# Column sums of a decoder trunk's norms written one item later than the split of their operand

## The chip, the cores and the metric

The kernel runs on one core of one Trainium2 chip. The metric is the device time of one execution in microseconds (us); lower is better. Matrix products run on TensorE (PE in the profile, its weight loads PEld), elementwise work on VectorE (DVE) and ScalarE (ACT), and all transfers between HBM and on-chip memory are issued by SyncE (SP).

## The reference

One layer of a hybrid decoder trunk, in float32, over 2048 tokens and 16 meta tokens put in front, 1024 channels:

```python
h = concat([meta, x])                       # (2064, 1024)
u = rmsnorm(h, mix_norm_g)
p = u @ w_in                                # 1024 -> 1792
p_pool, p_bval, p_bgate, p_cgate, p_cx = split(p)
y_a = pool_mixer(p_pool, ...)               # causal mean over windows 2, 4, 8, 16
y_b = conformer(p_bval, p_bgate, ...)       # gate, causal conv of 31 taps, LayerNorm over 256 channels, silu, matmul
y_c = rg_lru(p_cgate, p_cx, ...)            # causal conv of 4 taps, gates, linear scan, gelu gate
h = h + concat([y_a, y_b, y_c]) @ w_out
h = h + square(relu(rmsnorm(h, mlp_norm_g) @ w_up)) @ w_down     # 1024 -> 4096 -> 1024
return rmsnorm(h, final_norm_g)[meta:]
```

## The kernel before

Channels lie on the 128 partitions, tokens along the free dimension, so an activation of 1024 channels is eight blocks of 128 channels. The tokens are worked in four chunks of 512 (chunk 0 has the 16 meta tokens too).

Each float32 operand is split into a high part, rounded to the type fp32r, and a low rest: `split` (L109) makes the high part on ScalarE (L110) and the rest on VectorE (L111). A product is then three matmuls: high by high, high by low, low by high. An output block of 128 channels by 512 tokens takes 8 channel blocks x 3 = 24 matmuls (`mm_tile`, L278) into one PSUM bank of the pool pm, which has four. Weights come by DMA into tiles wr and are split into tiles wh, two items ahead.

A norm needs the sum of squares over channels, that is across partitions. VectorE adds the squared blocks into a tile ss (`add_square`, L345 and L346), `colsum` splits ss into a tile hl (one buffer) and multiplies it with a matrix of ones on TensorE: two matmuls, L327 for the high part and L328 for the low part, into the pool pb. `rsqrt_of` follows, a square root on ScalarE (L335) and a reciprocal on VectorE (L337).

The program is a list of items, each an output block with its products:

- W: a block of the input projection (14 a chunk), evacuated by `evac_w` (L448, or L454 for chunk 1, whose norm comes late: `gen_late`).
- O: a block of the output projection (8 a chunk). `evac_o` loads the residual into a tile xr (L712), adds it (L714) and squares the sum for norm 2.
- U: the MLP's first product, in four groups a chunk. Chunks 1 to 3 use a scheme with seven products instead of eight (`up_unit`, L302 and L820), with sums of weights that `gen_sums` makes during chunk 0 from loads of `w_up` (L194 to L204).
- D: the second product, 8 blocks a group; the first two run as a pair (`mm_pair`, L292), the second of them only evacuates.

The order is W of chunks 0 and 1 interleaved, O of chunk 0, three more W of chunk 1, then for each chunk its groups of U and D; O of the next chunk and W of the one after come behind the last D of chunks 0 and 1, and O of chunk 3 amid the last D of chunk 2.

All other work is in generators, run by `pump` after each item: it gives the item a budget (5000 for W and O, 3000 for D and for U of chunk 0, 150 for other U), takes the next generator step and subtracts the cost that the step yields, until the credit is used up. A debt is carried over to the next item; a credit is not. Generators in the list `urgent` run first, then the `Mix` of the next chunk, whose lanes take turns. The ones that matter here:

- `gen_x` (chunks 2, 3): eight steps of 1300, one for each block k: load the block into xr (L411), square it, scale and split it into a tile U (L148, L149); then the column sum and the root, 3500. It runs during O of the chunk before the one before.
- `gen_late` (chunk 1): eight loads and squares, 620 each, then the sum and 3500, then the scaling of the held W blocks. It runs during the first U of chunk 0.
- `gen_ln` (each chunk): the LayerNorm, with two column sums one after the other (mean, variance), steps of 1250, 1250, 1250, 3300 and 2500. Its outputs are two of the eight blocks that `gen_ysplit` splits for O.
- `gen_norm2` (`gen_norm2_0` for chunk 0): norm 2, 3300 and then the operands of U.
- `gen_final`: sum and root, 3300, then eight output steps of 660 (L860, output DMA L861).

The tile xr has two buffers, shared by `gen_x`, `gen_late` and `evac_o`. `need` and `need_mix` run a generator to its end at once, before an item that needs it; they don't look at the yielded cost.

The framework orders the instructions of each engine when the program is built: by the order in which they are written, but an instruction whose operands it expects to be late is put behind ready ones, and slots of tiles are given in that order. So a column sum may already stand amid the matmuls of the next item. At run time each engine keeps that order.

Of the kernel before, what the change touches and what calls it, by code (L numbers as in the profile page):

```python
# [31 lines left out]
D = 1024  # L32
KB = D // P
NT = 512
NCH = 4
# [18 lines left out]
BUD0 = 5000  # L54
BUD_U = 150
BUD_D = 3000
GELU_C = 0.7978845608028654


# [20 lines left out]
def build(nc, tc, x0, xr, w_in, w_out, w_fold, w_up, w_down, vecs, gates, pools, pws, out):  # L80
# [25 lines left out]
    def ps_back():  # L106
        return pb.tile([P, NT], F32, name=nm("pb"), tag="pb")
# [207 lines left out]
    def split_new(src):  # L315
        n = src.shape[-1]
        hl = t_("hl", (2, W0), HLB, F32R)
        hi, lo = hl[:, 0, :n], hl[:, 1, :n]
        split(hi, lo, src)
        return hi, lo  # L320

    def colsum(src):

        n = src.shape[-1]
        hi, lo = split_new(src)
        ps = ps_back()
        T.matmul(ps[:, :n], ones, hi, start=True, stop=False)  # L327
        T.matmul(ps[:, :n], ones, lo, start=False, stop=True)  # L328
        return ps
# [23 lines left out]
    for c in range(NCH):  # L353
        o = Chunk()
# [9 lines left out]
    def subs_of(o, full=True):  # L364
        if o.c == 0:
            return [(0, 264), (264, 528)] if full else [(META, W0)]
        return [(0, NT)]
# [35 lines left out]
    def gen_x(o):  # L403

        o.x = []
        if o.c > 1:
            ss = t_("ss", W0, 2)
        for k in range(KB):
            hl = a_tile()
            raw = t_("xr", NT, 2)  # L410
            nc.sync.dma_start(out=raw, in_=xr[o.c - 1, k])  # L411
            if o.c > 1:
                add_square(ss, raw, 0, NT, k == 0)
            split_to(hl[:, 0], hl[:, 1], raw, vc("g1", k))
            o.x.append(hl)
            yield 1300
        if o.c > 1:
            o.rs1 = rsqrt_of([colsum(ss[:, :NT])], subs_of(o), 1.0 / D)
            yield 3500

    def gen_late(o):

        ss = t_("ss", W0, 2)
        for k in range(KB):
            raw = t_("xr", NT, 2)
            nc.sync.dma_start(out=raw, in_=xr[o.c - 1, k])
            add_square(ss, raw, 0, NT, k == 0)
            yield 620
        o.rs1 = rsqrt_of([colsum(ss[:, :NT])], subs_of(o), 1.0 / D)
        yield 3500  # L430
        for kind, i, t in o.held:
            evac_w(o, kind, i, [t])
            yield 700
# [104 lines left out]
    def gen_ln(o):  # L538
        acc = [o.acc[0], o.acc[1]]
        sq = [o.ub[0], o.ub[1]]  # L540
        V.tensor_tensor(out=sq[0][:, :NT], in0=acc[0], in1=acc[1], op=ALU.add)
        ps = colsum(sq[0][:, :NT])
        yield 1250
        for i in range(2):
            V.scalar_tensor_tensor(out=acc[i], in0=ps, scalar=-1.0 / 256.0, in1=acc[i], op0=ALU.mult, op1=ALU.add)
            A.activation(out=sq[i][:, :NT], in_=acc[i], func=AF.Square)
        yield 1250
        V.tensor_tensor(out=sq[0][:, :NT], in0=sq[0][:, :NT], in1=sq[1][:, :NT], op=ALU.add)
        ps = colsum(sq[0][:, :NT])
        yield 1250  # L550
        rs = rsqrt_of([ps], [(0, NT)], 1.0 / 256.0)
        yield 3300
        for i in range(2):
            V.tensor_tensor(out=acc[i], in0=acc[i], in1=rs[:, :NT], op=ALU.mult)
            A.activation(out=acc[i], in_=acc[i], func=AF.Identity, scale=vc("lng", i), bias=vc("lnb", i))
            A.activation(out=sq[i][:, :NT], in_=acc[i], func=AF.Sigmoid)
            V.tensor_tensor(out=acc[i], in0=acc[i], in1=sq[i][:, :NT], op=ALU.mult)
            o.y[2 + i] = acc[i]
        yield 2500
# [157 lines left out]

    def gen_norm2(o):

        rs = rsqrt_of([colsum(o.ss2[:, :NT])], [(0, NT)], 1.0 / D)  # L720
        yield 3300
        o.u2 = ops = {n: [b_tile(), b_tile()] for n in ("B11", "T2", "T3", "T1", "B21", "T4", "B22")}
        free = [("s", SBF)] * SBF + [("t", TB)] * TB
# [53 lines left out]

    def gen_norm2_0(o):

        rs = rsqrt_of([colsum(o.ss2[:, :NT])], [(0, NT)], 1.0 / D)  # L780
        yield 3300
        o.u2 = []
        for k in range(KB):
            raw = t_("s", W0, SBF)[:, :NT] if k % 2 else t_("t", W0, TB)[:, :NT]
            V.scalar_tensor_tensor(out=raw, in0=o.h[k][:, :NT], scalar=vc("g2", k), in1=rs[:, :NT], op0=ALU.mult, op1=ALU.mult)
            t = b_tile()
            split(t[:, 0, :NT], t[:, 1, :NT], raw)
            o.u2.append(t)
            yield 1400
# [63 lines left out]
            add_square(o.ssf, h, s0, s1, j == 0)  # L853

    def gen_final(o, s0, s1):
        rs = rsqrt_of([colsum(o.ssf[:, s0:s1])], [(s0, s1)], 1.0 / D)
        yield 3300
        for k in range(KB):
            h = o.h[k][:, s0:s1]
            V.scalar_tensor_tensor(out=h, in0=h, scalar=vc("gf", k), in1=rs[:, s0:s1], op0=ALU.mult, op1=ALU.mult)  # L860
            nc.sync.dma_start(out=out[o.c, k, :, s0:s1], in_=h)  # L861
            yield 660
# [22 lines left out]
    credit = [0.0]  # L885

    def pump(budget):
        credit[0] = min(credit[0], 0) + budget
        while credit[0] > 0:
            v = step()  # L890
            if v is None:
                break
            credit[0] -= v

# [82 lines left out]
    for n, it in enumerate(items):  # L977
        kind, c, j, (s0, s1) = it
        o = ch[c]
# [140 lines left out]
```

## Time and profile before

| | |
|---|---|
| median of 3 runs | 1968.43 us (1966.31 to 1968.72) |
| the profiled execution | 1969.41 us |
| its span, first to last instruction | 1967.6 us |
| granted TensorE clock, mean | 0.996 |
| busy: PE, DVE, ACT | 1932.1, 1510.1, 1099.2 us |
| column sums (L327, L328) | 20 pairs of matmuls |

A row of the timeline gives the start and the length in us, engine, line, operation, output and inputs, shape and count; in brackets how long the engine was idle before it, and who released it. A row of the waits gives who waited for whom, the us in total, the times and the longest. In a table by stretches, each engine's busy time and count stand before the granted clock, the DMA share and GB/s. PE's busy time counts overlapping matmuls, so its lost time is better read from starts and ends of neighbouring rows.

### The profile page before, as it was taken

The numbers are of one execution on the slowest core, as the hardware profiler recorded it, in microseconds if no ns is written. First come the engines' busy times: TensorE is split into PE (matmuls) and PEld (weight loads), VectorE is DVE, ScalarE is ACT, GpSimd is POOL, SyncE is SP. The second block draws the span as 40 slices with busy tenths as digits, with TensorE's granted clock in tenths as the row PEclk, the third lists the DMA queues.
The fourth block names the chain that finished last, engine by engine and source line by source line (L and its number), as shares of the span: only waits on it lengthen the run. The fifth ranks groups of instructions, "written<-read, shape, count | busy, mean of one in ns | idle before, by whom it ended". The sixth has DMA issues, their size and how long they took to land.

```text
span 1967.6 us, 29715 instructions
## 1 busy us (share of the span) xinstructions
PE 1932.1 (98%) x10644; PEld 1664.2 (85%) x10644; DVE 1510.1 (77%) x2423; ACT 1099.2 (56%) x1839; POOL 0.2 (0%) x4
## 2 busy tenths in 40 slices
PE   8999999999999999999999999999999999999997
PEld 7888878878888789898898778988989889889897
DVE  7986689977756899985776799986768597656487
ACT  6575464646544536675575443775658356445374
POOL 0000000000000000000000000000000000000000
PEclk9999999999999999999999999999999999999999
DMA  5412456645855425353444543534435434545354
GB/s 196 137 43 76 129 168 221 206 160 171 275 164 162 143 92 168 90 166 109 147 132 125 184 124 107 152 112 144 140 116 163 132 102 150 173 135 154 108 178 143
DMA packets 160035, 285.07 MB, mean 145 GB/s; under 512 B 17552, under 2 KB 23824, under 8 KB 159888
## 3 DMA queue, kind: packets, MB, share of 16 engines
q1 hardware_dynamic: 159888, 283.18, 46.3%
q8 instruction: 83, 1.36, 0.3%
q14 instruction: 64, 0.52, 0.1%
HBM read 255.85 MB, written 27.26 MB: 144 GB/s over the span
## 4 chain that ended last, share of the span: by engine, by line
PE 82%; DVE 9%; DMA 4%; ACT 2%; issue 2%; SPq 0%; DVEq 0%; ACTq 0%
PE pm L278 52%; PE pm L302 11%; PE pw L302 9%; PE pm L292 8%; DVE wh L111 2%; DMA xr<-d_xr 2%; DVE ca L534 1%; DMA s<-d_w_up 1%; DVE fr L820 1%; DVE t L568 1%; PE pb L311 0%; ACT wh L110 0%; DMA wr<-d_w_down 0%; DVE U L149 0%; PE pb L312 0%
## 5 line engine op out<-in xcount | busy, mean ns | idle before, releaser
L110 ACT ACTIVATE wh<-wr 128x512 fp32r<-128x512 f32 x828 | 517.3, 627 | 713.8 <-PE pm L278 490.5
L278 PE MATMUL pm<-U,wh 128*128 128x512 f32 (+1 forms) x3504 | 788.0, 384 | 1.7 <-DVE wh L111 1.7
L278 PEld LDWEIGHTS pm<-U,wh 128*128 128x128 f32 x3504 | 634.9, 188 | 142.4 <-DVE wh L111 2.2
L111 DVE TENSOR_TENSOR wh<-wr,wh 128x512 fp32r<-128x512 f32 x828 | 566.5, 688 | 209.0 <-ACT wh L110 204.4
L278 PE MATMUL pm<-H,wh 128*128 128x512 f32 (+1 forms) x2112 | 449.9, 372 | 9.6 <-ACT H L390 7.3
L278 PEld LDWEIGHTS pm<-H,wh 128*128 128x128 f32 x2112 | 370.8, 190 | 84.1 <-ACT H L390 7.3
L302 PE MATMUL pm<-H,wh 128*128 128x256 f32 x2304 | 292.3, 282 | 2.3 <-DVE wh L111 1.4
L302 PEld LDWEIGHTS pm<-H,wh 128*128 128x128 f32 x2304 | 282.2, 188 | 5.2 <-DVE wh L111 2.2
L302 PE MATMUL pw<-H,wh 128*128 128x256 f32 x1728 | 223.2, 283 | 1.6 <-DVE fr L820 1.6
L302 PEld LDWEIGHTS pw<-H,wh 128*128 128x128 f32 x1728 | 212.0, 189 | 4.7 <-DVE fr L820 4.0
L292 PE MATMUL pm<-U,wh 128*128 128x512 f32 (+1 forms) x768 | 176.2, 388 | 0.0
L292 PEld LDWEIGHTS pm<-U,wh 128*128 128x128 f32 x768 | 140.2, 188 | 31.0 <-DVE wh L111 0.3
L534 DVE SCALAR_TENSOR_TENSOR ca<-Pbv,vec,ca 128x512 f32<-128x512 f32 x180 | 127.8, 745 | 0.0
L849 DVE TENSOR_TENSOR h<-h,pm 128x512 f32<-128x512 f32 (+1 forms) x106 | 71.5, 674 | 60.5 <-PE pm L278 45.6
L794 DVE TENSOR_TENSOR U<-fr,U 128x512 fp32r<-128x512 f32 x128 | 87.5, 685 | 11.4 <-ACT fr L793 11.4
L792 ACT ACTIVATE U<-fr 128x512 fp32r<-128x512 f32 x128 | 79.6, 624 | 1.9
L793 ACT ACTIVATE fr<-fr 128x512 f32<-128x512 f32 x128 | 79.3, 621 | 1.1
L820 DVE TENSOR_TENSOR fr<-pw,fr 128x512 f32<-128x512 f32 x96 | 66.0, 687 | 4.5 <-PE pw L302 1.9
L346 DVE TENSOR_TENSOR ss<-ss,fr 128x512 f32<-128x512 f32 (+1 forms) x84 | 54.2, 645 | 17.5 <-ACT fr L345 16.8
L337 DVE RECIPROCAL rs<-rs 128x512 f32<-128x512 f32 (+2 forms) x17 | 53.9, 3169 | 10.7 <-ACT rs L335 10.6
L534 DVE SCALAR_TENSOR_TENSOR ca<-h,vec,ca 128x512 f32<-128x512 f32 x60 | 42.7, 746 | 0.0
L840 ACT ACTIVATE fr<-fr 128x512 f32<-128x512 f32 x48 | 30.0, 624 | 12.2 <-DVE fr L839 11.8
(206 smaller groups left out, 1151.5 us busy)
## 6 DMA issues: line engine op xcount, KB each, us to landing
wr<-d_w_down SPq DMA_DIRECT2D x272, 256.0 KB, 2.9
wr<-d_w_up SPq DMA_DIRECT2D x208, 256.0 KB, 2.9
wr<-sums SPq DMA_DIRECT2D x192, 256.0 KB, 3.3
wr<-d_w_in SPq DMA_DIRECT2D x92, 256.0 KB, 2.8
xr<-d_xr SPq DMA_DIRECT2D x56, 256.0 KB, 2.9
wr<-wo_fold SPq DMA_DIRECT2D x32, 256.0 KB, 2.7
wr<-d_w_out SPq DMA_DIRECT2D x32, 256.0 KB, 2.6
s<-d_w_up SPq DMA_DIRECT2D x32, 256.0 KB, 3.8
```

Source lines behind the costliest of these rows:

```text
L110: A.activation(out=hi, in_=src, func=AF.Copy)
L111: V.tensor_tensor(out=lo, in0=src, in1=hi.bitcast(F32), op=ALU.subtract)
L278: T.matmul(ps[:, : s1 - s0], w[k // 4][:, a, (k % 4) * P : (k % 4 + 1) * P], rhs[k][:, b, s0:s1], start=(k == 0 and j == 0), stop=(k == KB ...
L292: T.matmul(ps[:, : s1 - s0], w[k // 4][:, a, (k % 4) * P : (k % 4 + 1) * P], rhs[k][:, b, s0:s1], start=(k == 0 and j == 0), stop=(k == KB ...
L302: T.matmul(ps, w[:, a, k * P : (k + 1) * P], op[k // 2][:, b, (k % 2) * 256 : (k % 2) * 256 + 256], start=(k == 0 and j == 0), stop=(k == ...
L346: V.tensor_tensor(out=ss[:, c0:c1], in0=ss[:, c0:c1], in1=sq[:, c0:c1], op=ALU.add)
L534: V.scalar_tensor_tensor(out=a, in0=o.ub[i][:, k : k + NT], scalar=vc("cw", i * CONVK + k), in1=a, op0=ALU.mult, op1=ALU.add)
L792: A.activation(out=f[:, 0], in_=r, func=AF.Square)
L793: A.activation(out=r, in_=r, func=AF.Square)
L794: V.tensor_tensor(out=f[:, 1], in0=r, in1=f[:, 0].bitcast(F32), op=ALU.subtract)
L820: V.tensor_tensor(out=out.rearrange("p (a c) -> p a c", a=2), in0=ps.rearrange("p (a c) -> p a c", a=2), in1=x.unsqueeze(1).broadcast_to([ ...
L849: V.tensor_tensor(out=h, in0=h, in1=ps[:, : s1 - s0], op=ALU.add)
```

## The change

`colsum` becomes a generator: it writes the split, yields the mark NEXT_ITEM, and only when it is resumed takes its PSUM tile and writes the two matmuls; the root follows behind them. `pump` ends at the mark and sets the credit to zero, so the rest is written after the matmuls of the next item. This holds for 16 of the 20 sums: eight of the LayerNorms, the input norms of chunks 1, 2 and 3, norm 2 of chunks 1 and 2, and the final norms of chunks 0 to 2. Norm 2 of chunks 0 and 3 and the two halves of the last final norm are written as before. In `need` and `need_mix` the mark makes no pause.

```diff
-    def colsum(src):
+    def colsum(src, wait=True):
         n = src.shape[-1]
         hi, lo = split_new(src)
+        if wait:
+            yield NEXT_ITEM
         ps = ps_back()
         T.matmul(ps[:, :n], ones, hi, start=True, stop=False)
         T.matmul(ps[:, :n], ones, lo, start=False, stop=True)
...
     def gen_x(o):
-            o.rs1 = rsqrt_of([colsum(ss[:, :NT])], subs_of(o), 1.0 / D)
+            o.rs1 = rsqrt_of([(yield from colsum(ss[:, :NT]))], subs_of(o), 1.0 / D)
...
     def gen_ln(o):
-        ps = colsum(sq[0][:, :NT])
+        ps = yield from colsum(sq[0][:, :NT])
...
     def gen_norm2(o):
-        rs = rsqrt_of([colsum(o.ss2[:, :NT])], [(0, NT)], 1.0 / D)
+        rs = rsqrt_of([(yield from colsum(o.ss2[:, :NT], 0 < o.c < NCH - 1))], [(0, NT)], 1.0 / D)
...
     def gen_final(o, s0, s1):
-        rs = rsqrt_of([colsum(o.ssf[:, s0:s1])], [(s0, s1)], 1.0 / D)
+        rs = rsqrt_of([(yield from colsum(o.ssf[:, s0:s1], o.c < NCH - 1))], [(s0, s1)], 1.0 / D)
...
     def pump(budget):
         credit[0] = min(credit[0], 0) + budget
         while credit[0] > 0:
             v = step()
             if v is None:
                 break
+            if v == NEXT_ITEM:
+                credit[0] = 0.0
+                break
             credit[0] -= v
```

`gen_late` and both sums of `gen_ln` change as `gen_x` and the first of `gen_ln` do.

More of the change, by code (lines that the diff above doesn't have):

```diff
@@ L56 @@
 BUD_D = 3000
+NEXT_ITEM = -1
 GELU_C = 0.7978845608028654
@@ L428, in gen_late @@
             yield 620
-        o.rs1 = rsqrt_of([colsum(ss[:, :NT])], subs_of(o), 1.0 / D)
+        o.rs1 = rsqrt_of([(yield from colsum(ss[:, :NT]))], subs_of(o), 1.0 / D)
         yield 3500
@@ L548, in gen_ln @@
         V.tensor_tensor(out=sq[0][:, :NT], in0=sq[0][:, :NT], in1=sq[1][:, :NT], op=ALU.add)
-        ps = colsum(sq[0][:, :NT])
+        ps = yield from colsum(sq[0][:, :NT])
         yield 1250
@@ L778, in gen_norm2_0 @@
     def gen_norm2_0(o):
-        rs = rsqrt_of([colsum(o.ss2[:, :NT])], [(0, NT)], 1.0 / D)
+        rs = rsqrt_of([(yield from colsum(o.ss2[:, :NT], 0 < o.c < NCH - 1))], [(0, NT)], 1.0 / D)
         yield 3300
```

## The prediction

> **What bounds the kernel now.** I read the page first, then TensorE's list of waits, then its timeline at the places where it waits, then the order of the other queues there.
>
> ```profile
> PE 1932.1 (98%) x10644; PEld 1664.2 (85%) x10644; DVE 1510.1 (77%) x2423; ACT 1099.2 (56%) x1839; POOL 0.2 (0%) x4
> ...
> PE pb L327 <- ACT hl L110: 7.1, 4, 1.9
> ...
> PE pb L328 <- DVE hl L111: 0.9, 2, 0.7
> ...
> 1446.91 11.16 PE pm L278 x48
> ```
>
> TensorE is the bound: 98% busy. The second row, from its list of waits, says that the first matmul of a column sum (L327) waited four times, 7.1 us in all, for ScalarE's half of its split. The third is the same for the second matmul (L328) and VectorE's half: twice, 0.9. The last, from the chain of work, is the pace at full speed: 11.16 / 48 = 0.2325 us for a matmul of 512 columns, so 5.58 us for an item of 24. Of those four waits, one (at 1955 us, 1.9) is the last sum of the kernel, which the change leaves as it is. The other three are the prize. TensorE's timeline at each:
>
> ```profile
> 263.69 1.32 PE L278 MATMUL pm<-H,wh 128*128 128x512 f32 x5
> 266.54 0.50 PE L327 MATMUL pb<-hl,ones 128*128 128x512 f32 x1 [1.54 <-ACT hl L110]
> 266.88 0.63 PE L278 MATMUL pm<-H,wh 128*128 128x512 f32 x2
> 267.34 0.42 PE L328 MATMUL pb<-hl,ones 128*128 128x512 f32 x1
> 267.61 1.56 PE L278 MATMUL pm<-H,wh 128*128 128x512 f32 x6
> ...
> 266.52 0.69 DVE L111 TENSOR_TENSOR hl<-ss,hl 128x512 fp32r<-128x512 f32 x1 [0.23 <-ACT hl L110]
> ...
> 647.72 2.48 PE L278 MATMUL pm<-H,wh 128*128 128x512 f32 x10
> 652.01 0.50 PE L327 MATMUL pb<-hl,ones 128*128 128x512 f32 x1 [1.81 <-ACT hl L110]
> 653.16 0.50 PE L328 MATMUL pb<-hl,ones 128*128 128x512 f32 x1 [0.65 <-DVE hl L111]
> 654.47 7.33 PE L278 MATMUL pm<-H,wh 128*128 128x512 f32 x24 [0.80 <-DVE h L714]
> 661.63 1.56 PE L278 MATMUL pm<-U,wh 128*128 128x512 f32 x6
> ...
> 1128.70 1.33 PE L278 MATMUL pm<-H,wh 128*128 128x512 f32 x5
> 1131.82 0.52 PE L327 MATMUL pb<-hl,ones 128*128 128x512 f32 x1 [1.80 <-ACT hl L110]
> 1132.55 0.79 PE L328 MATMUL pb<-hl,ones 128*128 128x512 f32 x1 [0.21 <-DVE hl L111]
> 1133.15 6.94 PE L278 MATMUL pm<-H,wh 128*128 128x512 f32 x24
> 1139.99 0.74 PE L278 MATMUL pm<-U,wh 128*128 128x512 f32 x2
> ```
>
> Call them A (late input norm of chunk 1), B and C (input norms of chunks 2 and 3, amid the O items of chunks 1 and 2). Loss at A: from 265.01 to 267.61 is 2.60 us with four matmuls' work in it (0.93; two L278 run between the sums), so 1.67. At B: 650.20 to 654.47 is 4.27, less the two sums' own 0.46: 3.81; then 24 matmuls take 654.47 to 661.63, 7.16 for 5.58: 1.58 more. Together 5.39. At C: 3.12 less 0.46 is 2.66, and 6.84 for 5.58 is 1.26: 3.92. All three: 10.98 us, the ceiling of what this change can bring.
>
> The slow matmuls behind B and C are the clock, in a table by stretches (PE busy and count, then the granted clock):
>
> ```profile
> 267.60:271.00 3.40, 3.40 (x16) 1.00 0.20 74
> ...
> 654.40:657.70 3.30, 3.23 (x8) 0.50 0.47 147
> ...
> 1130.00:1133.10 3.10, 1.09 (x3) 0.85 0.63 180
> 1133.10:1135.50 2.40, 2.40 (x7) 0.50 0.68 224
> ```
>
> After A's 1.54 us of idling the clock stayed at 1.00; after B and C it was 0.50 for some 3 us. [...]
>
> **The change part by part.** No instruction is added or removed. Sixteen pairs of matmuls, with the root and reciprocal that follow, are written one item later than their split, and at each of them the pump gives up the rest of its budget. So two effects: the sums' place in TensorE's order, and the place of all the steps behind.
>
> *What is behind the wait at B and C.* Taking a wait from TensorE's queue helps only if the next instruction is ready. At B it was not: L278 at 654.47 waited for the evacuation L714, whose xr load landed last. SyncE's xr loads there, and the piece of the chain:
>
> ```profile
> 617.51 0.33 SPq L411 DMA_DIRECT2D xr<-d_xr  x1
> 629.92 1.00 SPq L411 DMA_DIRECT2D xr<-d_xr  x2
> ...
> 636.67 0.33 SPq L712 DMA_DIRECT2D xr<-d_xr  x1
> 640.57 0.93 SPq L411 DMA_DIRECT2D xr<-d_xr  x2
> 645.34 1.59 SPq L411 DMA_DIRECT2D xr<-d_xr  x2
> 650.67 1.59 SPq L712 DMA_DIRECT2D xr<-d_xr  x2
> ...
> 650.67 3.03 DMA xr<-d_xr
> ```
>
> (One L411 load at 634.8 is left out.) xr has two buffers, shared by gen_x (L411) and the evacuation of O items (L712). O item 3 gets its load at 650.67, behind all eight of gen_x; with four pm banks O item 7 cannot start before item 3 is evacuated. So the lost credit matters more than the sum's place. By the yields: before, the pump of the last D item (3000) takes the final norm's sum, root and reciprocal (3300); O0's takes 8 outputs (8 x 660); O1's loads k0 to k3 (4 x 1300); O2's k4 to k7; O3's the sum. That is the order of the rows. After, the last D item stops at the split; O0's pump (5000) takes 3300 and 3 outputs, and is left at -280; O1's (4720) 5 outputs, k0, k1, left at -1180; O2's (3820) k2 to k4, left at -80; O3's (4920) k5 to k7 and the split; O4's the sum. In the queue for xr, O2's load comes third instead of fifth after O1's, and O3's seventh instead of tenth. From 617.51 to 650.67 nine loads went by, 3.7 us each. So O3's load is issued about 3 x 3.7 = 11 us sooner, near 640, O3 is evacuated near 643, and O7 at 650.2 finds its bank free. O4's load keeps its place, eleventh; it is evacuated some us before the first W item wants the bank, near 656. C has the same yields. So at B and C the second wait goes too, and with it the half clock.
>
> What is late next: the sum itself. Its split ends when k7 is squared and split, which the new order leaves near 651 at B, and the place that the sum gets among O7's matmuls was 1.81 us too early in the row before. I take a residual between 0 and 1.81, half of it: B 5.39 - 0.9 = 4.5, C 3.92 - 0.9 = 3.0. Ends: 0 (the psum wait stays) and 5.39 or 3.92.
>
> *A.* The sum is written behind the rest of its U item. Six matmuls (267.61 to the item's end) come first, from 265.01 to 266.40; the high half is ready for 266.54, the low half ends at 267.21 (266.52 + 0.69). Residual 0.14 + 0.58 = 0.7: a gain of 1.0. Ends 0 and 1.67.
>
> *LayerNorm of chunk 0.* This is where the change costs. Rows of its two sums, its last product and split, and O's start:
>
> ```profile
> 158.03 0.39 PE L327 MATMUL pb<-hl,ones 128*128 128x512 f32 x1
> ...
> 164.64 0.40 PE L328 MATMUL pb<-hl,ones 128*128 128x512 f32 x1
> ...
> 177.62 0.69 DVE L557 TENSOR_TENSOR ca<-ca,h 128x512 f32<-128x512 f32 x1
> ...
> 182.90 0.62 ACT L110 ACTIVATE H<-ca 128x512 fp32r<-128x512 f32 x1
> ...
> 183.65 1.28 DVE L111 TENSOR_TENSOR H<-ca,H 128x512 fp32r<-128x512 f32 x2
> ...
> 181.34 30.88 PE L278 MATMUL pm<-H,wh 128*128 128x512 f32 x132
> ```
>
> Both sums are written in the pump of W(0,12), the outputs in W(1,12)'s, with W(0,13), W(1,13) and W(1,2) behind as cover. After: split in W(0,12)'s, first sum in W(1,12)'s, second in W(0,13)'s, outputs in W(1,13)'s: two items later, and W(1,2) alone covers. The first sum moves behind W(1,12), the second behind W(0,13), to about 170.3 for 164.64. From there to the end of L557 it took 178.31 - 164.64 = 13.67, so 184.0; a split without a queue (0.62 + 0.69) ends at 185.3. O at 181.34 has 12 matmuls that don't need these operands (blocks 0 and 1 of O0 and O1), until 184.1. I take a loss of 2 us: 1.2 and some queueing. Ends: 0, as the split rows stand already behind L557 by several us, and 12.4 (full two items, 11.2, with 1.2). No other work covers it.
>
> *LayerNorms of chunks 1 to 3, norm 2 of chunks 1 and 2.* Their sums (six and two) show no wait on TensorE in the list, so nothing is gained; the two waits for the second half are B's 0.65 and C's 0.21. Nothing lost either: norm 2 is covered by 14 W items (14 x 5.58 = 78 us, and its steps need six items' budget), the LayerNorms by the mix steps and y splits that follow, at least four items. *Final norms* of chunks 0 to 2 only write outputs; their effect is the xr order above.
>
> *The weight sums of U (gen_sums).* One stall is set by their loads standing in VectorE's queue ahead of a weight split:
>
> ```profile
> 396.31 0.69 DVE L196 TENSOR_TENSOR s<-t,s 128x512 f32<-128x512 f32 x1 [2.03 <-DMA s<-d_w_up]
> ...
> 398.32 3.99 PE L278 MATMUL pm<-U,wh 128*128 128x512 f32 x16 [1.73 <-DVE wh L111]
> ```
>
> Three units (s5 to s7) are begun within one pair of D items there. The credit lost in chunk 1's late norm shifts it: by the yields the second group is spread, and the first (s1 to s3, near 305 us) is bunched as the second was. The stall of 1.73 moves: 0 in the sum, ends +1.73 and -1.73.
>
> Sum: 4.5 + 3.0 + 1.0 - 2.0 = 6.5 us. The profiled execution took 1969.41 (span 1967.6, 1.8 around it), 0.98 over the median 1968.43 of the runs. 1969.41 - 6.5 = 1962.9; on the median's footing 1961.9. I predict 1962.
>
> **The rivals.** *The psum wait stays (28%).* If SyncE's xr order is not spread, TensorE waits at B and C for L714 as now, the sums lose their free place in the gap (0.46 each) and only A gains: 1.0 - 0.9 - 2.0 = -1.9, so 1970.3, or 1968.3 without the chunk 0 loss. For it: the 0.80 wait for L714 in B's row. Against: the row order of the loads follows the yields exactly, and those change. *Slower: chunk 0's LayerNorm slips by its full two items (12%).* TensorE stands in front of O for 12.4 us; with A to C recovered as above (8.5) the time is 1968.4 + 3.9 = 1972.3, up to 1974 with the half clock behind it, priced by B's 1.58. It decides from an operand ready at 192.6 on (184.1 + 8.5). For it: today the split ends at 184.93 with no cover left. Against: the chain behind the second sum starts 5.6 later, not 11.2. *Everything recovered (7%):* no residual, no loss at O: 1968.4 - 11 = 1957.5. *Nothing moves (3%):* the sums were already issued amid the next item's matmuls at most places, as at 267.34, so the written place would not matter: 1968.4.
>
> **How the numbers follow.** The forecast has 50%, gains of 4 to 9 us, its own range 1959.5 to 1964.5. A measurement of this kernel tells about 0.2%, 3.9 us. Faster: 50 + 7 = 57%; same 28 + 3 = 31%; slower 12%. The range must take in the psum rival: 1957.5 to 1970.5.
>
> **What would show it.** Right: no TensorE wait at O7 of chunks 1 and 2, clock 1.00 there, three L411 loads between L712s, L714 of O3 near 643; a short stand at the start of O in chunk 0 near 184, for H. Wrong: a wait for L714 in place of L327 (the order did not spread), a stand of more than 4 us near 184, or a new wait for wh near 310 to 335 without the one at 398 going away.

## The result, and the profile after

The change made the kernel slower: 1981.9 us, median of 6 runs (1980.07 to 1982.92), against 1968.45 (6 runs of the kernel before on the same chip), ratio 1.0065 with an interval of 1.0055 to 1.0075. The profiled execution took 1981.34 us, its span 1979.6. Forecast were 1962.0 and at most 1970.5. In what follows line numbers are those of the changed kernel: one more than before up to the split in `colsum`, three more behind it (L327 is L330, L714 is L717). Rows of other runs carry the lines of their own kernels.

The page's busy times, then TensorE's list of waits:

```profile
PE 1936.1 (98%) x10644; PEld 1666.8 (84%) x10644; DVE 1509.0 (76%) x2423; ACT 1110.3 (56%) x1847; POOL 0.2 (0%) x4
```

```profile
PE pb L330 <- ACT hl L111: 7.6, 4, 2.8
...
PE pm L279 <- ACT H L111: 6.8, 3, 2.8
...
PE pm L279 <- DVE H L112: 1.0, 1, 1.0
```

Two things to see. The wait for a split, which the change was to shorten (7.1 us before), is 7.6. And there is a new row, 6.8 us in three waits put down to ScalarE's part of an operand H. Only the first of the three, 1.21 us at O of chunk 0, is one for H. The two of 2.79 us stand ahead of matmuls on U, among the W items: both end 0.15 us behind the end of an evacuation (L451, 701.94 and 1184.92 us), and in e2 the same stop is put down to that line. They are waits for a PSUM bank. ScalarE has eight instructions more than before (1847 for 1839) and 11.1 us more of work, although the change adds no instruction; I come back to that. TensorE's timeline at the places of the prediction and at the new waits:

```profile
180.70 2.94 PE L279 MATMUL pm<-H,wh 128*128 128x512 f32 x12
184.85 0.73 PE L279 MATMUL pm<-H,wh 128*128 128x512 f32 x2 [1.21 <-ACT H L111]
186.63 7.62 PE L279 MATMUL pm<-H,wh 128*128 128x512 f32 x25 [1.04 <-DVE H L112]
...
270.04 0.50 PE L330 MATMUL pb<-hl,ones 128*128 128x512 f32 x1 [1.47 <-ACT hl L111]
...
658.05 0.50 PE L330 MATMUL pb<-hl,ones 128*128 128x512 f32 x1 [1.37 <-ACT hl L111]
...
659.79 0.40 PE L331 MATMUL pb<-hl,ones 128*128 128x512 f32 x1
...
702.09 10.15 PE L279 MATMUL pm<-U,wh 128*128 128x512 f32 x36 [2.79 <-ACT H L111]
...
1139.84 0.80 PE L330 MATMUL pb<-hl,ones 128*128 128x512 f32 x1 [2.81 <-ACT hl L111]
...
1185.07 5.14 PE L279 MATMUL pm<-U,wh 128*128 128x512 f32 x21 [2.79 <-ACT H L111]
```

A (270) waits as before. B (658) has lost its waits for the second half and for the evacuation. C (1139) waits longer than before. New are two stops at the start of O in chunk 0 (184.85, 186.63), and one of 2.79 us among the W items of chunk 2 (702) and of chunk 3 (1185). The granted clock there is the last but two number of each row:

```profile
187.00:189.00 2.00, 2.00 (x6) 1.62 (x5) 0.27 (x2) 0.09 (x1) 0.00 (x0) 0.50 0.04 8
...
654.00:658.00 4.00, 2.69 (x12) 1.86 (x10) 2.34 (x5) 2.29 (x5) 0.00 (x0) 1.00 0.68 216
...
702.00:704.00 2.00, 1.91 (x5) 1.60 (x6) 2.00 (x5) 2.00 (x6) 0.00 (x0) 0.59 0.32 115
...
1139.00:1142.00 3.00, 2.16 (x5) 1.77 (x6) 3.00 (x5) 1.40 (x4) 0.00 (x0) 0.55 0.38 117
```

To have the whole account I set TensorE's k-th matmul of a kernel beside the k-th of the kernel before (both issue 10644) and noted by how much it starts later. What that difference gains across a stretch is the loss there. The stretches are named by their times in the kernel before; "400" is the stall of the weight sums. All runs of this study are in the table, one profiled execution each, with the median of the timed runs and their ratio to the kernel before, run beside them (its medians: 1968.05 to 1969.3). A dot is less than 0.25 us. Of the 12.0 us between the two spans, 11.1 are in the table and 0.9 lie behind the last matmuls. Where the cells of a row don't add up to its end, the rest lies outside these stretches: in the first 163 us alone the kernels differ from the kernel before by -1.6 to +2.1 us.

| run (sums written late) | O, chunk 0 163-193 | 400 378-415 | B 636-674 | W, chunk 2 693-725 | C 1112-1161 | W, chunk 3 1172-1196 | U, chunk 2 1297-1422 | U, chunk 3 1615-1673 | end | median, us | ratio (interval) |
|---|---|---|---|---|---|---|---|---|---|---|---|
| the change | +4.1 | -1.6 | -4.1 | +4.5 | . | +3.0 | +1.9 | +3.3 | +11.1 | 1981.9 | 1.0065 (1.0055-1.0075) |
| e1 norm 2 | . | -1.1 | -1.0 | . | . | . | . | . | -2.1 | 1968.78 | 1.0000 (0.9990-1.0010) |
| e2 final norms | . | -1.8 | -3.9 | +4.5 | -2.7 | . | +1.9 | . | -0.3 | 1967.5 | 0.9993 (0.9983-1.0003) |
| e3 input norms | . | -2.1 | +0.6 | . | -0.4 | . | . | . | -2.4 | 1967.67 | 0.9994 (0.9982-1.0005) |
| e4 LayerNorms | +4.1 | -0.8 | . | . | +2.0 | . | +0.3 | +3.3 | +9.8 | 1977.66 | 1.0041 (1.0025-1.0056) |
| e5 LayerNorm of chunk 0 | +2.6 | -2.1 | -0.7 | . | +0.6 | . | . | . | +2.8 | 1973.11 | 1.0024 (1.0015-1.0033) |
| e13 LayerNorms 1 to 3 | . | -1.3 | +0.4 | . | +2.6 | . | . | +3.3 | +5.4 | 1974.09 | 1.0025 (1.0014-1.0036) |
| e9 all but LayerNorms | . | . | -4.1 | +2.9 | -2.8 | . | +1.9 | . | -3.2 | 1969.28 | 1.0008 (0.9998-1.0019) |
| e6 LayerNorms, no Sigmoid | +1.3 | -1.8 | +0.7 | . | . | . | . | . | +2.1 | 1972.19 | 1.0014 (1.0002-1.0025) |
| e7 none, no Sigmoid | . | -1.1 | . | . | -0.9 | . | . | . | +0.8 | 1973.27 | 1.0023 (1.0012-1.0033) |
| e14 the change, no Sigmoid | +1.3 | . | -3.6 | +5.7 | -3.1 | . | +1.9 | . | +4.7 | 1968.11 | 1.0001 (0.9990-1.0012) |
| e15 none, two loads at norm 2 | . | -0.5 | -0.7 | . | . | . | . | +3.6 | +6.2 | 1972.11 | 1.0020 (1.0010-1.0030) |
| e17 LayerNorms, one Sqrt more | +4.1 | -0.8 | -2.1 | . | -1.0 | . | . | . | +1.7 | 1971.84 | 1.0018 (1.0010-1.0027) |
| e18 the change, two Sqrt more | +4.1 | -2.1 | -4.7 | +3.0 | -2.4 | . | +1.8 | . | +1.5 | 1970.96 | 1.0011 (1.0003-1.0020) |
| e19 none, one load at O | +1.0 | -0.4 | -2.2 | . | -1.3 | . | . | . | +2.0 | 1970.68 | 1.0012 (1.0001-1.0022) |
| e12 input norms behind W | . | -1.3 | -0.5 | . | +2.0 | . | . | . | +1.3 | 1970.09 | 1.0008 (0.9999-1.0018) |
| e8 final norms, prior W | . | -0.8 | -1.3 | . | -2.0 | . | +1.9 | . | +0.8 | 1966.36 | 0.9984 (0.9974-0.9994) |
| e10 and input norms behind W | . | -0.6 | -4.5 | . | -2.3 | . | +1.9 | . | -5.2 | 1963.05 | 0.9976 (0.9966-0.9987) |
| e11 and the late norm | . | -2.1 | -4.9 | . | -2.5 | . | +2.0 | . | -7.6 | 1961.45 | 0.9965 (0.9954-0.9976) |

How far to trust a cell: at 400, B and C kernels that touch nothing there differ by up to 2 us (e1 and e19 at B, e5 and e19 at C), so a single cell of 1 or 2 us says little in these. At B and C most of that is the clock: the kernel before has one piece of half clock at B (0.50 from 654.3 to 657.7 us) and one at C (0.50 from 1132.2 to 1135.6), and a piece more or less is worth about 1.6 us (the last section). The columns of O, both W and both U stay within 0.3 us where nothing is touched, and the argument rests on them; where a stop stands, the clock behind it moves them too (O 2.6 or 4.1, W of chunk 2 2.9, 4.5 or 5.7).

### The profile page after: what moved, and what is told of

Read it like the earlier page. It is cut to its first block, busy times and chain, and to the rows that moved or that the text cites. A ratio compares the mean times of both kernels' runs of the same rounds, so it can differ in the third digit from the quotient of the medians.

```text
span 1979.6 us, 29717 instructions
## 1 busy us (share of the span) xinstructions
PE 1936.1 (98%) x10644; PEld 1666.8 (84%) x10644; DVE 1509.0 (76%) x2423; ACT 1110.3 (56%) x1847; POOL 0.2 (0%) x4
## 4 chain that ended last, share of the span: by engine, by line
PE 79%; DVE 9%; DMA 4%; ACT 4%; issue 3%; SPq 0%; DVEq 0%; ACTq 0%
PE pm L279 50%; PE pm L303 11%; PE pw L303 9%; PE pm L293 8%; DVE wh L112 2%; DMA xr<-d_xr 2%; DVE ca L537 2%; DMA s<-d_w_up 1%; ACT wh L111 1%; DVE fr L823 1%; PE pb L312 0%; DMA t<-d_w_up 0%; DVE t L571 0%; DMA wr<-d_w_down 0%; DVE U L150 0%
## 5 line engine op out<-in xcount | busy, mean ns | idle before, releaser
L852 DVE TENSOR_TENSOR h<-h,pm 128x512 f32<-128x512 f32 (+1 forms) x106 | 71.7, 676 | 65.6 <-PE pm L279 50.6
```

The costliest lines, as they stand in the source:

```text
L852: V.tensor_tensor(out=h, in0=h, in1=ps[:, : s1 - s0], op=ALU.add)
```

## The experiments

Each diff is against the changed kernel. `colsum(src, False)` writes the sum at once, as before the change.

**Which group of sums costs: e1 to e4.** One group of sums is late in each; for e2, as an example, the others go back:

```diff
-        ps = yield from colsum(sq[0][:, :NT])
+        ps = yield from colsum(sq[0][:, :NT], False)
... (both sums of gen_ln; likewise gen_x, gen_late, gen_norm2)
```

> Only norm 2 of chunks 1 and 2 has its sum one item late; the other 14 sums are written as before. Theory (each delayed group costs or gains at its own place, and the places add): the W items of chunks 2 and 3 lose what they lost in the changed kernel, 4.6 us near 699 us and 3.1 us near 1182 us, with a TensorE stop of some 3 us at each; B and C stay as before: 1968.4 + 7.7 = 1976 us. Rival (any shift reshuffles the whole order, and the stalls fall anywhere): no stop at those two places in particular, 1966 to 1971 us.

> Only the final norms of chunks 0 to 2 have their sums one item late. Theory (the credit lost at the final norm spreads the xr loads): O7 of chunk 1 no longer waits for a PSUM bank and the clock stays at 1.00 there, B gains 4.2 us although its own sum is written as before; the sum itself still waits 1 to 2 us; C gains about nothing, as in the changed kernel: 1964 us. Rival (B's gain came from the late writing of the input norm's own sum): no gain, 1968 us. Rival (reshuffled order): anything from 1965 to 1972 with stalls at new places.

> Only the input norms of chunks 1, 2 and 3 have their sums one item late. Theory: the xr loads keep their order, so B and C still wait for the bank that the xr load holds, with the half clock behind; only the stop near 398 us goes, 1.7 us, since chunk 1's late norm shifts the weight sums: 1967 us. Rival (B's gain is that of its own sum): 1968.4 - 4.2 - 1.7 = 1962.5 us.

> Only the eight LayerNorm sums are one item late. Theory: TensorE stands in front of O of chunk 0, near 183 to 187 us, for the LayerNorm outputs, with the half clock behind: 4.2 us; the LayerNorms of chunks 1 to 3 cost at most the 1.9 us lost amid U of chunk 2: 1972.6 us, up to 1974.5. Rival (reshuffled order): 1968 plus or minus 3, with stops elsewhere.

With norm 2 alone there is no stop at 699 or 1182 us: my first theory after the result was wrong. But e1 does not show that a late sum of norm 2 is free. Its sums did not move: all 10644 matmuls stand in the order of the kernel before, and only VectorE and ScalarE have some steps in another order. The final norms alone bring B's and C's gain, 3.9 and 2.7, as their credit spreads the xr transfers, and give it back among the W items of chunk 2 (+4.5) and in U of chunk 2 (+1.9), so that e2 missed its theory. The input norms alone do nothing at A, B and C: there too the three sums stand behind as many matmuls as before. The LayerNorms alone cost 8 us, more than the 4 to 6 expected.

**Which LayerNorms: e5 and e13.** `gen_ln` late for chunk 0 only, and for chunks 1 to 3 only:

```diff
-        ps = yield from colsum(sq[0][:, :NT])
+        ps = yield from colsum(sq[0][:, :NT], o.c == 0)
```

> Only the LayerNorm sums of chunk 0 are one item late; every other sum stands as before. All eight LayerNorm sums together gave 1977.66 us against 1969.2 (ratio 1.0041). Theory (chunk 0's LayerNorm, which stands on the way to the items of O, carries about half of it): the two stops of TensorE near 184.5 and 186.4 us with the half clock behind them are here too, +4.2 us by the alignment of TensorE's instructions, and nothing is lost later: 1972 to 1974 us. Rival (the loss is that of the LayerNorms of chunks 1 to 3 alone, and what is lost at O is recovered by the norms' next wait): 1968 to 1970 us.

> Only the LayerNorm sums of chunks 1 to 3 are one item late. All eight gave +8 us, those of chunk 0 alone +4.7. Theory (the two parts stand at different places and add): +3 to +4 us, 1971 to 1973 us, with no stops at 184 to 187 us and with norm 2 of chunk 3 late by 2 to 3.5 us beyond what TensorE is late. Rival (the later chunks lose only because chunk 0 had shifted the order behind it): 1967 to 1970 us.

Both parts cost, +4.7 and +4.9 us by the ratios, and they add to somewhat more than e4's 8.1, within the intervals. By the columns: 2.6 at O of chunk 0, and 3.3 in U of chunk 3.

**All but the LayerNorms: e9.** `gen_ln` as before, everything else late.

> The change without its LayerNorm part: the sums of the input norms, of norm 2 of chunks 1 and 2 and of the final norms of chunks 0 to 2 are late, the eight LayerNorm sums stand as before. Theory (the LayerNorm part is what costs; of the rest each part alone gave 1967.5 to 1968.8 us): 1966 to 1970 us. Rival (the parts cost more together than alone: norm 2 and final norms late together give the stop at the W items of chunk 3, 1182 us, that neither gave alone): 1971 to 1975 us, with stops of about 2.9 us near 695 and near 1180.

It is +0.8 per mille, not told from no change, so the LayerNorm part carries most of the loss. The stop among the W items of chunk 2 is there, that of chunk 3 is not; it comes only with the LayerNorms late as well, and the rival is half wrong.

**Is it the tables: e6, e7, e14.** The changed kernel has 72 ACT_TABLE_LOADs, the kernel before 64. Each stands directly ahead of a Sigmoid, a Sqrt, an Exp or a Tanh on ScalarE, and in neither trace is one function loaded twice in a row. By line, the root's and the LayerNorm's Sigmoid's, first of the kernel before, then of the changed one (the shortest, the median and the longest in ns, then the first and the last start in us):

```profile
L335 ACT ACT_TABLE_LOAD  x4: 1283/1283/1283, 23.8 to 614.1; - x4
...
L556 ACT ACT_TABLE_LOAD  x4: 1283/1283/1283, 173.8 to 1479.8; - x4
```

```profile
L338 ACT ACT_TABLE_LOAD  x8: 1283/1283/1283, 23.7 to 1589.7; - x8
...
L559 ACT ACT_TABLE_LOAD  x4: 1283/1283/1283, 180.3 to 1495.0; - x4
```

Each takes 1.283 us. Of the four more at the root, the last is norm 2 of chunk 3 (1589.7), where the kernel before has none behind 614.1. Its cause is the LayerNorm's Sigmoid (L559): before, its last load was at 1479.8, a root of `gen_rg` had a load at 1484.2, and norm 2's root at 1582.83 has none; written later, the Sigmoid came behind that root, with its load at 1495.0, and the next load is that at norm 2's root. A first test replaced the Sigmoid, so these three kernels leave out that part of silu:

```diff
-            A.activation(out=sq[i][:, :NT], in_=acc[i], func=AF.Sigmoid)
+            A.activation(out=sq[i][:, :NT], in_=acc[i], func=AF.Square)
```

> All eight LayerNorm sums are one item late, as in the run of the LayerNorm sums alone (1977.66 us). The LayerNorm's Sigmoid is replaced by a Square of the same shape, so the kernel leaves out that part of silu and ScalarE needs no Sigmoid table there. To be read against the twin kernel with the sums where they were. Theory (the late sums put the roots and the Sigmoids of different chains in another order, and the added ACT_TABLE_LOADs of about 1.28 us on the chains are most of the loss): this minus twin is 2 to 4 us, what is left at O of chunk 0. Rival (the places of the sums alone do it): this minus twin stays at 7 to 10 us.

> The twin: the LayerNorm's Sigmoid is a Square as well, and all sums stand as in the kernel before. Theory on table loads: a few of the 64 ACT_TABLE_LOADs go, those of the Sigmoid and of the root behind it, 8 or fewer; they stand beside other work on TensorE, so 1966 to 1969 us. Rival (ScalarE's table loads set the end already in the kernel before): 1955 to 1963 us.

> The whole change, with the LayerNorm's Sigmoid replaced by a Square of the same shape (it leaves out that part of silu). The whole change is +13 us, the change without its LayerNorm part +1.6, and the late LayerNorm sums without a Sigmoid were no slower than their twin (1972.2 against 1973.3 us). Theory (the LayerNorm part loses by the tables that its Sigmoid brings): 1970 to 1975 us, and no ACT_TABLE_LOAD at the root of norm 2 of chunk 3. Rival (the whole change loses by the places of its sums together, whatever the tables): 1979 to 1984 us.

The late LayerNorms cost nothing against their twin (1972.2 and 1973.3), and the whole change with that edit is level with the kernel before. The twin itself moved by +4.5 us, against both of its expectations and with no column to show for it (its profiled execution, 1970.40 us, is one of its fastest), so this edit is not a clean one. And e14's profiled execution, 1973.74 us, keeps the stop among the W items of chunk 2. The next three leave the Sigmoid where it is.

**Table loads put in, and one moved away: e15, e17, e18.** e15 writes every sum as before and brings a load to the root of norm 2 of chunk 3, by a Sigmoid of one column that needs a load of its own. e17 has all LayerNorm sums late and moves the load of that root to a Sqrt of one column, soon after the LayerNorm; e18 does so in the whole change, for chunks 2 and 3.

```diff
 e15, gen_norm2
+        if o.c == 3:
+            rs = t_("rs", W0, 2)
+            A.activation(out=rs[:, :1], in_=o.ss2[:, :1], func=AF.Sigmoid)
+            ps = yield from colsum(o.ss2[:, :NT], False)
... (the root into rs and its reciprocal as in rsqrt_of; all other sums False)
 e17 (o.c == 3) and e18 (o.c > 1), end of gen_ln
+        if o.c > 1:
+            A.activation(out=sq[1][:, :1], in_=sq[1][:, :1], func=AF.Sqrt)
         yield 2500
```

> The kernel before with one added ScalarE instruction: a Sigmoid of one column, ahead of norm 2 of chunk 3, into the tile that the root then overwrites. It brings the ACT_TABLE_LOAD at that root which the late LayerNorm sums brought, and with it an order of VectorE in which the addition of a D item stands ahead of the reciprocal. Nothing else is moved. Theory (the 3.3 us lost in U of chunk 3 come of this load: 0.7 us at the root, 2 us at the reciprocal that waits behind an addition whose matmuls are not done, and the rest behind them): +2 to +3.5 us, 1970 to 1972 us, all of it between 1582 and 1660 us. Rival (that loss was the late sums' own): 0 to +0.7 us.

> All eight LayerNorm sums late (1977.66 us), and one added ScalarE instruction behind the last LayerNorm's Sigmoid: a Sqrt of one column, which brings the table of the roots back some 90 us before norm 2 of chunk 3 needs it. Theory (the load at that root and the order of VectorE behind it are the 3.3 us lost in U of chunk 3): 2 to 3.5 us less than with the late sums alone, 1974 to 1976 us, and the reciprocal stands right behind the root again. Rival (the late sums' own places): 1977 to 1978.5 us.

> The whole change with one added ScalarE instruction behind the LayerNorm's last Sigmoid in chunks 2 and 3: a Sqrt of one column, which brings the table of the roots back before norm 2 of chunk 3 and the input norm of chunk 3 need it. Nothing is left out. The whole change took 1981.9 us (+13). Theory (extra ACT_TABLE_LOADs on the chains, and the orders that they bring, are most of the loss): the 3.3 us in U of chunk 3 go, and 1 to 3 us at the input norm and the W items of chunk 3; what is lost at O of chunk 0 (4.2) and in the W items of chunk 2 (4.6) stays: 1974 to 1978 us. Rival (the places of the sums in the whole change, whatever the tables): 1979.5 to 1983 us.

e15's two loads, the Sigmoid's at 1582.74 ahead of the sum's split and the root's at 1587.87, cost the kernel before 0.2% (3.9 us; 3.6 in the column of U of chunk 3). That the 3.6 meets the changed kernel's 3.3 is luck: 2.1 of it stand ahead of a piece of half clock, 1623.4 to 1626.8 us, that the changed kernel does not have there, and the rest comes from there on. One added Sqrt takes the late LayerNorms' loss there from 3.3 to nothing (the median falls by 5.8, more than expected; the intervals of e4 and e17 just meet). Two added Sqrt take the whole change from 1981.9 to 1971.0, with all 16 sums late and nothing left out. That is more than I expected of e18: the stop among the W items of chunk 3 went too.

Where a load of 1.28 us becomes more is seen on VectorE. The changed kernel at norm 2 of chunk 3, VectorE then ScalarE:

```profile
1592.39 0.69 DVE L852 TENSOR_TENSOR h<-h,pm 128x512 f32<-128x512 f32 x1 [1.98 <-PE pm L279]
1593.10 0.69 DVE L112 TENSOR_TENSOR wh<-wr,wh 128x512 fp32r<-128x512 f32 x1
1593.71 3.35 DVE L340 RECIPROCAL rs<-rs 128x512 f32<-128x512 f32 x1
...
1589.70 1.28 ACT L338 ACT_TABLE_LOAD   x1
1591.00 0.69 ACT L338 ACTIVATE rs<-pb,eps 128x512 f32<-128x512 f32 x1
```

The root ends at 1591.69, the reciprocal starts at 1593.71, 2.0 us later. My reading is that with the load the root looked later to the framework, so it put a D item's addition (L852) and a weight split ahead of the reciprocal in VectorE's order; the addition waits for its matmuls. The same place in e15 and in e17:

```profile
1587.17 0.69 DVE L859 TENSOR_TENSOR h<-h,pm 128x512 f32<-128x512 f32 x1 [1.02 <-PE pm L279]
1587.89 0.69 DVE L112 TENSOR_TENSOR wh<-wr,wh 128x512 fp32r<-128x512 f32 x1
1589.89 3.35 DVE L728 RECIPROCAL rs<-rs 128x512 f32<-128x512 f32 x1 [1.31 <-ACT rs L727]
```

```profile
1583.88 0.69 DVE L112 TENSOR_TENSOR wh<-wr,wh 128x512 fp32r<-128x512 f32 x1
1585.17 3.35 DVE L340 RECIPROCAL rs<-rs 128x512 f32<-128x512 f32 x1 [0.59 <-ACT rs L338]
```

e15 has the changed kernel's order from loads alone, but there the addition holds nothing up: the reciprocal waits 1.31 us more for the root itself. e17, with late sums, has the reciprocal right behind the root. So what carries the claim is e17, and e15 shows only that loads in front of this root cost. In the W items of chunk 3 it is the same play. The changed kernel there, two ScalarE rows and two of VectorE:

```profile
1155.02 1.28 ACT L473 ACT_TABLE_LOAD   x1
...
1156.96 1.28 ACT L338 ACT_TABLE_LOAD   x1
...
1173.08 0.69 DVE L451 TENSOR_TENSOR Pbv<-pm,rs 128x512 f32<-128x512 f32 x1
...
1184.24 0.68 DVE L451 TENSOR_TENSOR Pcx<-pm,rs 128x512 f32<-128x512 f32 x1
```

A gate's Sigmoid (L473) stands ahead of norm 2's root, which then needs a load of its own. Norm 2's steps come late and close together, and between two evacuations (L451) VectorE works 11.2 us at nothing but them and weight splits. TensorE is out of PSUM banks and waits until the second one, 1185.07. In e18 the root comes first, at 1151.52, with one load, the Sigmoid's, behind it:

```profile
1151.52 0.69 ACT L338 ACTIVATE rs<-pb,eps 128x512 f32<-128x512 f32 x1 [1.35 <-PE pb L331]
...
1152.74 1.28 ACT L473 ACT_TABLE_LOAD   x1
```

and TensorE has no stop there. That the order at this place hangs on the Sqrt added far ahead of it is shown by e18 (in e14, without the LayerNorm's Sigmoid, the stop is gone too); the single steps of the framework between the two were not followed.

**The stop among the W items of chunk 2: e8.** The evacuations of chunks 2 and 3 with priority, the final norms late, all else as before:

```diff
-            evac_w(o, wk, i, mm_tile(w, o.x, subs_of(o, wk != "z")))
+            pss = mm_tile(w, o.x, subs_of(o, wk != "z"))
+            if c > 1:
+                with tc.high_priority(EARLY):
+                    evac_w(o, wk, i, pss)
+            else:
+                evac_w(o, wk, i, pss)
```

> The final norms' sums are one item late for chunks 0 to 2, all other sums stand as before, and the evacuations of the W items of chunks 2 and 3 are placed with priority, so ahead of norm 2's steps in the order of VectorE and ScalarE. With the final norms alone the time was 1967.5 us: 3.9 us gained at the input norm of chunk 2, 2.5 to 2.9 at that of chunk 3, and 4.6 lost at 692.6 us, where TensorE waited 2.95 us for an evacuation. Theory (the evacuation stood behind norm 2's steps in VectorE's queue): the stop at 692.6 us goes, nothing takes its place, 1962 to 1965 us. Rival (VectorE is nearly full there, and what is put off comes due at the start of U): 1966 to 1969 us, with a stop behind the last W item that waits for an operand of norm 2.

TensorE without and with the priority (e2, then e8):

```profile
695.78 7.61 PE L279 MATMUL pm<-U,wh 128*128 128x512 f32 x25 [2.79 <-DVE Pbv L451]
```

```profile
676.85 35.47 PE L279 MATMUL pm<-U,wh 128*128 128x512 f32 x152
```

The stop is gone, no other stands behind the last W item, and the kernel is faster than before for the first time. The time is in the rival's range all the same: U of chunk 2 keeps its +1.9, and in this profile B brought only 1.3. The +1.9 (1.3 to 1.4 of it are left at 1430 us) is in every kernel with late final norms and in no other; what brings it was not followed, so its cause is open.

The two loads of W of chunk 3 stand here as well. The changed kernel:

```profile
671.94 1.28 ACT L473 ACT_TABLE_LOAD   x1
...
673.89 1.28 ACT L338 ACT_TABLE_LOAD   x1
```

The first is a gate's Sigmoid's, the second that of norm 2's root, which needs none in the kernel before. All five kernels with the stop have this pair (the change, e2, e9, e14, e18). e8 and e10 have it too, without the stop. So the pair alone does not bring the stop, the evacuations' place has to allow it; whether the stop would go without the pair was not tested.

**The place of the input norms' sums: e12, e10, e11.** The sum of chunks 2 and 3 is written behind the matmuls of the first W item (which sets `w0`), in e12 alone, in e10 on top of e8. e11 adds three items of delay for the late norm of chunk 1.

```diff
+    def gen_xs(o):
+        hi, lo = split_new(o.ss1[:, :NT])
+        while not o.w0:
+            yield NEXT_ITEM
+        ps = ps_back()
...
 e11, gen_late
+        for _ in range(3):
+            yield NEXT_ITEM
```

> Only the sums of the input norms of chunks 2 and 3 are written behind the first W item's matmuls, all else is as in the kernel before, the xr transfers too. Theory (the wait at the sum and the wait for the bank behind it have different causes: the place of the sum, and the order of the xr transfers): the waits for the split at 650 and 1130 us (1.8 to 2.0 us and 0.9 us behind each) go, the wait for the evacuation of O (0.8 to 1.1 us) stays or grows by up to what the sum no longer waits: 1964 to 1967 us. Rival (the evacuation of O was late all along and the sum's wait only stood in front of it): that wait grows to 3 us or more, 1968 to 1970 us.

> Built on the kernel with late final norms and prior evacuations of the W items of chunks 2 and 3 (1966.4 us): the sums of the input norms of chunks 2 and 3 are written behind the matmuls of the first W item (24 matmuls, some 5 us, later than in the change). Theory (one item was too short: the sum was still written into the last O item, ahead of the time at which ScalarE had copied its high part, so TensorE waited 1.3 to 2.7 us for it at 655 us and 2 us at 1133 us): both waits go, 3.5 to 5 us less, 1961.5 to 1963.5 us. Rival (the norm is now on the path, because the evacuations of the first W items wait for it and the PSUM banks run out): a stop of 1 to 4 us for a bank within the first four W items, 1965 to 1969 us.

> As the run before it, with the sum of the late input norm of chunk 1 (264 us) three items later than its split instead of at once. Theory (the same cause: 1.5 to 2.1 us of waiting for ScalarE's copy there, in the kernel before and with one item's delay alike): the wait at 264 us goes, 1.5 to 2 us less than the run before it, 1960 to 1962 us. Rival (what is gained there is taken back by the next wait for weights, near 400 or 556 us): no difference from the run before it, within 0.5 us by the profile's alignment at 600 us.

e12 at B:

```profile
651.15 0.50 PE L429 MATMUL pb<-hl,ones 128*128 128x512 f32 x1 [1.42 <-ACT hl L111]
652.30 0.49 PE L430 MATMUL pb<-hl,ones 128*128 128x512 f32 x1 [0.65 <-DVE hl L112]
653.56 7.28 PE L279 MATMUL pm<-H,wh 128*128 128x512 f32 x24 [0.77 <-DVE h L727]
```

Written behind a later item, the sum still ran ahead of the last O item (the 24 matmuls on H), behind as many matmuls as in the kernel before: probably the framework expects that item to wait for its bank, by the xr transfers, and puts the sum first. So e12 did not test what it was made for, and it fits e1 and e3: the written place is not the place. With the xr transfers spread (e10, e11) the sums at B and C do move, by 48 matmuls, and in e11 the one at A by 27. e11:

```profile
270.23 0.39 PE L446 MATMUL pb<-hl,ones 128*128 128x512 f32 x1
...
659.07 0.39 PE L429 MATMUL pb<-hl,ones 128*128 128x512 f32 x1
...
1134.97 0.39 PE L429 MATMUL pb<-hl,ones 128*128 128x512 f32 x1
```

No bracket at A, B or C: TensorE waits for none of the three. Both times are where the theory had them. e11 takes 1961.45 us, 0.35% less than the kernel before, and is the best version found.

**A load at O of chunk 0: e19.**

```diff
             V.tensor_tensor(out=acc[i], in0=acc[i], in1=rs[:, :NT], op=ALU.mult)
+            if o.c == 0 and i == 0:
+                A.activation(out=sq[0][:, :1], in_=acc[0][:, :1], func=AF.Tanh)
```

> The kernel before with one added ScalarE instruction in the LayerNorm of chunk 0: a Tanh of one column between the root and the Sigmoid, which brings there the ACT_TABLE_LOAD that the late sums brought by their order. No sum is moved. Theory (table loads are a part of the 4.2 us lost at O of chunk 0, and the two items' delay is the other): a stop of 0.5 to 1.5 us at 184 to 187 us, 1969 to 1971.5 us. Rival (the delay of the two sums alone does it): no stop there, 1968 to 1969 us. Rival (the load alone does it): two stops and matmuls at half clock as with the late sums, 1972 to 1974 us.

One stop instead of two, 0.85 us, at full clock:

```profile
185.53 8.85 PE L279 MATMUL pm<-H,wh 128*128 128x512 f32 x37 [0.85 <-ACT H L111]
```

So a load there costs about 1 us, as the first theory had it. The rest of the 4.1 fits the delay of the two sums (e6, without the Sigmoid's load, has 1.3) and the half clock (1.5).

## Why the prediction was wrong, point by point

The forecast's sum was -6.5 us, the account gives +11.1.

- *A, forecast 1.0 gained, got nothing.* This step failed: "The sum is written behind the rest of its U item" was true of the text, not of TensorE's order. The sum stands behind exactly as many matmuls as before, and the wait is 1.47 for 1.54. Three items of delay move it and remove the wait (e11). The rival "nothing moves", given 3%, held here.
- *B, forecast 4.5, got 4.1.* Right in mechanism; the size is in part luck. The transfers spread, three L414 between two L715:

```profile
633.75 0.34 SPq L715 DMA_DIRECT2D xr<-d_xr  x1
...
636.09 0.33 SPq L414 DMA_DIRECT2D xr<-d_xr  x1
...
638.84 0.33 SPq L414 DMA_DIRECT2D xr<-d_xr  x1
...
642.09 0.33 SPq L414 DMA_DIRECT2D xr<-d_xr  x1
...
643.96 0.33 SPq L715 DMA_DIRECT2D xr<-d_xr  x1
```

  The load of O item 3 went 6.7 us sooner (643.96 for 650.67) where I had 11; that was enough, TensorE no longer waits for the evacuation, and the clock stayed at 1.00. But the half clock, 1.58 of the forecast's 5.39, can go without the waits: e17 and e19 keep all three waits at B, have full clock all the same, and gain 2.1 and 2.2. So some 2 of the 4.1 are the transfers'. That the lost credit matters more than the sum's place was right: e2, which leaves the input norms alone, gains as much.
- *C, forecast 3.0, got nothing.* e2, e8, e9 and e10 gain 2.0 to 2.8 there; e7, e17 and e19, which leave C's sum alone and have full clock there, gain 0.9 to 1.3. In the whole change the sum waits 2.81 for its split and the clock falls to 0.55, which gives it all back; in e18 the wait is 1.72, the clock stays at 1.00 and 2.4 are there. With C's spread of 2 us between profiles I don't call a cause shown.
- *LayerNorm of chunk 0, forecast a loss of 2, got 4.1.* The place was right, a stand near 184 for H. By the timeline the last product ended at 184.2, where I had 184.0. But its split ended at 187.2 and not at 185.3: three other splits stood ahead of it on VectorE. That gave two stops, 2.25 us of idling, and then a half clock, 1.5 us, which I had priced for the rival alone. Without the half clock, in e5, it is 2.6: the term was mis-sized by 0.6, and the clock added the rest.
- *LayerNorms of chunks 1 to 3: "nothing lost either", got 3.3.* This step failed. I asked whether the sums and what follows them had time, which they had. I did not ask what their later place does to the order of ScalarE's functions; "no instruction is added or removed" left out the eight loads. A load of 1.28 us came before a root on whose result U of chunk 3 waits, and VectorE's order changed with it; with the load moved away the loss is gone (e17).
- *Norm 2 "covered by 14 W items", the final norms "only write outputs": got 4.5 in W of chunk 2, 3.0 in W of chunk 3 and 1.9 in U of chunk 2.* This is the step that failed most. The 14 items cover norm 2's own steps, but not the evacuations that stand among them on VectorE: TensorE came out of B earlier, norm 2's reciprocal came later (675.2 us in e2 for 671.0), and TensorE ran out of banks. Each of the forecast's gains had to pass this place. In W of chunk 3 the loads' order did it (e18). In W of chunk 2 VectorE's order is needed, since priority removes the stop (e8), and the same pair of loads stands there. The 1.9 in U of chunk 2 stays open.
- *The weight sums, forecast 0 with ends of 1.73, got -1.6*, within its ends; e1 to e4, which differ in what they delay, show -0.8 to -2.1 at this stall, and e1 has every matmul in its old place, so it is not this change's own.

The rivals: none came as a whole. The slower one put a stand of 12.4 us at O; it was 2.25, 4.1 with the clock. Losses of 2 to 4.5 us at four other places, each behind a gain or an operand I had declared covered, were in no case of mine.

## What to carry to other kernels

Before moving a step that contains a table function, list the loads of ScalarE's tables in the trace by line and time, and ask which function will be the last one before each root on the path: two Sqrt of one column, put where ScalarE has time, took back 11 of 13 us here. A gain on the bounding engine is only kept if the engine that empties its banks has room next: look at the evacuations behind the place, not at the moved step alone. Where a framework orders the queues by its own expected times, a later line in the text need not be a later place; count in the trace behind how many matmuls the step stands, before any time is read as its effect.

## What the runs showed of the hardware

All 72 table loads of the changed kernel and all 64 of the kernel before took 1283 ns, and the instruction behind one can start 1.30 us after the load's start (1589.70 to 1591.00).

The same idling did not always bring the same clock. e5 has the changed kernel's two stops at O of chunk 0, 1.21 and 1.04 us, and kept its clock at 1.00; the changed kernel fell to 0.50 behind them. The changed kernel, then e5:

```profile
183.60:186.90 3.30, 1.05 (x4) 0.57 (x4) 3.30 (x6) 1.72 (x4) 0.00 (x0) 1.00 0.30 79
187.00:190.30 3.30, 3.30 (x9) 2.62 (x8) 0.96 (x3) 0.63 (x1) 0.00 (x0) 0.50 0.02 5
190.40:193.70 3.30, 3.30 (x16) 2.68 (x15) 1.26 (x2) 1.16 (x2) 0.00 (x0) 1.00 0.29 79
```

```profile
183.20:186.40 3.20, 1.99 (x8) 1.05 (x6) 3.20 (x6) 3.03 (x6) 0.00 (x0) 1.00 0.25 64
186.60:189.80 3.20, 2.27 (x10) 1.87 (x11) 1.71 (x5) 0.63 (x1) 0.00 (x0) 1.00 0.03 7
```

The changed kernel alone has both: behind its stop of 2.79 us at W of chunk 2 the clock is 0.59 (702 to 704 us), behind the one of 2.79 us at W of chunk 3 it is 1.00 (1185 to 1188 us). Behind A's wait of 1.47 us it stayed at 1.00 (269 to 272 us). What decides between the two was not shown.

At O the two clocks make 1.5 us of difference from the same waits (4.1 and 2.6 in the table). W of chunk 2 shows it as well: its stop of 2.79 us costs 2.9 to 3.0 with no half clock behind it (e9, e18), 4.5 with one piece of it (the change, e2) and 5.7 with two (e14). So the half clock behind waits of 2 to 3 us is better carried as a chance than as a term, and a difference of about 1.6 us between two profiles is no effect of an edit until their clocks have been compared.
